# An ifftshift by DMA alone: the last strip split into small copies of 15 rows down to 2

## The chip, the cores and the metric

The kernel runs on one core of one Trainium2 chip. The metric is device time in microseconds (us), lower is better. A time is that of a whole execution; the profile is taken from one further execution, and its span runs from the first to the last instruction of the program. Nothing is computed: all work is done by the core's 16 DMA engines, which copy from one DRAM tensor to another.

## The reference

```python
def setup_inputs():
    return {"x": np.random.randn(8192, 8192).astype(np.float32)}

def reference(x):
    return np.fft.ifftshift(x)
```

For an even size this swaps the quadrants: element (r, c) of the output is element ((r + 4096) mod 8192, (c + 4096) mod 8192) of x. The tensor has 8192 rows of 32 KB, 268.4 MB in all, and each byte is read once and written once.

## The kernel before

R and C are 8192, hr and hc are 4096. A loop over `row` steps through the output in blocks of 512 rows, 16 blocks in all. In each block two DMAs are issued: the SP queue (`nc.sync`) copies the left half of the 512 output rows from the right half of the source rows, and the ACT queue (`nc.scalar`) copies the right half from the left half. Each DMA moves 512 half rows of 16 KB, 8 MB. Its access pattern, `dims`, has an outer dimension of 16 rows that follow each other (`ENGINES`), a middle one of 32 (`per`) with a step of 16 rows, and an inner one of 4096 contiguous floats.

So there are 32 DMAs, 16 on each queue, and no other work. The loop is inside a tile context, which does two things that are not seen in the code. It gives the DMAs eight semaphores in turn, four to each queue, and from the fifth DMA of a queue on it lets the issue wait until the DMA that last used the same semaphore has landed. And at the end it lets SP wait for all eight semaphores before the final barrier of the engines. Within a queue the DMAs run in the order of their issue; between the queues nothing sets an order.

Of the kernel before, what the change touches and what calls it, by code (L numbers as in the profile page):

```python
# [1 line left out]

# [4 lines left out]


ENGINES = 16


@with_exitstack
def kernel(
    ctx: ExitStack,
    tc: tile.TileContext,
    x: bass.AP,
    out: bass.AP,
):
    nc = tc.nc
    R, C = x.shape  # L20
    hr = R // 2
    hc = C // 2


    per = 32
    dims = [[C, ENGINES], [ENGINES * C, per], [1, hc]]
    for row in range(0, R, ENGINES * per):
        src_row = (row + hr) % R
        for queue, h in ((nc.sync, 0), (nc.scalar, hc)):
            queue.dma_start(  # L30
                out=bass.AP(out.tensor, out.offset + row * C + h, dims),
                in_=bass.AP(x.tensor, x.offset + src_row * C + hc - h, dims),
            )


# [1 line left out]
_INS = ['x']  # L37
_OUTS = [((8192, 8192), 'float32')]


def kernel(**inputs):
    import numpy as _np
    import concourse.bacc as _bacc
    import concourse.tile as _tile
    from concourse import mybir as _mybir
    from concourse.bass_utils import run_bass_kernel_spmd as _run

    nc = _bacc.Bacc("TRN2", target_bir_lowering=False, num_devices=1)  # L48
    arrays, args = {}, []
    for name in _INS:  # L50
        a = _np.ascontiguousarray(inputs[name])
        if a.dtype.kind in "iu":
            a = a.astype(_np.int64)
        arrays[f"in_{name}_dram"] = a
        args.append(nc.dram_tensor(f"in_{name}_dram", a.shape, _mybir.dt.from_np(a.dtype), kind="ExternalInput").ap())
    for i, (shape, dtype) in enumerate(_OUTS):
        dt = _mybir.dt.from_np(_np.dtype(dtype))
        args.append(nc.dram_tensor(f"out_{i}_dram", shape, dt, kind="ExternalOutput").ap())
    with _tile.TileContext(nc) as tc:
        kernel(tc, *args)  # L60
    r = _run(nc, [arrays], core_ids=[0])
    got = tuple(r.results[0][f"out_{i}_dram"] for i in range(len(_OUTS)))
    return got[0]
```

## Time and profile before

| what | value |
|---|---|
| three runs | 821.38, 823.50, 823.81 us; median 823.5 |
| span of the profiled execution | 821.2 us |
| DMAs | 16 on SP's queue (q1), 16 on ACT's (q10), 8192 KB each |
| median time from issue to landing | 204.0 us (SP), 204.1 us (ACT) |
| bytes moved | 268.44 MB, mean 327 GB/s |
| HBM read and written | 268.44 MB each, 654 GB/s over the span |

The profiled execution's own time is not given beside its span; the three times lie 0.2 to 2.6 us above it. A DMA is broken into packets, each of which is moved by one DMA engine. The profile has a record of each packet with its queue, bytes, start and duration, but not the number of its engine. A completion packet of 4 bytes raises a semaphore once an engine has done its share. The issuing instruction occupies only the queue of SP or ACT; it is not counted as busy time. In the view of stretches, PEclk is the clock of TensorE, which has no work here, the DMA share is the time of the packets that start in the stretch divided by sixteen times its length, and the rate counts their bytes.

### The profile page before, as it was taken

Reading aid. Unit: us, or ns where it says so; the run is one execution under the profiler, and the core shown is the slowest. Engines: PE = TensorE matmul, PEld = TensorE weight load, DVE = VectorE, ACT = ScalarE, POOL = GpSimd, SP = SyncE. Lnnn points to the kernel's source line nnn. Section 1 sums busy time; section 2 is a strip of 40 time slices with the busy share of each in tenths; the row PEclk is TensorE's granted clock in tenths of the full one; section 3 lists DMA queues with packets and bytes.
Section 4 is the critical chain, followed back from the end, with each engine's and each line's share of the span. In section 5 each row is a group of like instructions: output and inputs, shape, how many; then the busy total and the mean of one; then the engine's idle time right before and its main releaser. Section 6 shows DMA issues by size and latency. Waiting matters only on the chain. (4 is left out here: it accounts for less than half of the span.)

```text
span 821.2 us, 77 instructions
## 1 busy us (share of the span) xinstructions
POOL 0.2 (0%) x4
## 2 busy tenths in 40 slices
POOL 0000000000000000000000000000000000000000
DMA  8999999999999999999999999999999999999998
GB/s 296 333 324 329 331 328 334 330 330 329 327 330 329 331 326 332 332 327 328 330 330 330 330 323 330 324 330 330 332 326 329 330 322 333 329 329 327 330 329 276
DMA packets 16896, 268.44 MB, mean 327 GB/s; under 512 B 512, under 2 KB 512, under 8 KB 512
## 3 DMA queue, kind: packets, MB, share of 16 engines
q1 hardware_dynamic: 8448, 134.22, 50.2%
q10 hardware_dynamic: 8448, 134.22, 49.0%
HBM read 268.44 MB, written 268.44 MB: 654 GB/s over the span
## 5 line engine op out<-in xcount | busy, mean ns | idle before, releaser
L48 POOL MEMSET const-bfloat16-1.0<- 128x1 bf16 x1 | 0.1, 102 | 0.0
L48 POOL MEMSET const-uint8-127<- 128x1 uint8 x1 | 0.1, 102 | 0.0
L48 POOL MEMSET const-float32-0.0<- 128x1 f32 x1 | 0.1, 99 | 0.2 <-issue 0.2
L48 POOL MEMSET const-float32-1.0<- 128x1 f32 x1 | 0.1, 99 | 0.0
## 6 DMA issues: line engine op xcount, KB each, us to landing
out_dram<-in_x_dram ACTq DMA_DIRECT2D x16, 8192.0 KB, 204.1
out_dram<-in_x_dram SPq DMA_DIRECT2D x16, 8192.0 KB, 204.0
```

The costliest lines, as they stand in the source:

```text
L48: nc = _bacc.Bacc("TRN2", target_bir_lowering=False, num_devices=1)
```

## The change

The loop goes into a critical section of the tile context, in which the kernel does its own synchronization: every DMA raises one semaphore, `copied`, by 16 when it is done, and SP waits at the end until it has reached 16 times the number of DMAs, 62 x 16 = 992. The waits between the DMAs are gone.

SP's 16 DMAs are as before. ACT's first 15 are too. Its sixteenth is split. The first 384 rows of the last block go as one DMA of half rows (16 x 24 x 4096). Of the last 128 rows, one DMA moves the right 3584 floats of the half row (16 x 8 x 3584), and the strip that is left, 512 floats (2 KB) of each of the 128 rows, is moved by 29 DMAs: one of 9 rows, and then, for k from 15 down to 2, two of k rows each, the first with 256 + 8k floats of each row and the second with the other 256 - 8k. 9 + 15 + 14 + ... + 2 is 128.

```diff
+    with tc.tile_critical():
+        copied = nc.alloc_semaphore("copied")
+        n = 0
 
-    per = 32
-    dims = [[C, ENGINES], [ENGINES * C, per], [1, hc]]
-    for row in range(0, R, ENGINES * per):
-        src_row = (row + hr) % R
-        for queue, h in ((nc.sync, 0), (nc.scalar, hc)):
+        def copy(queue, row, col, dims):
+            nonlocal n
+            src = (row + hr) % R * C + (col + hc) % C
             queue.dma_start(
-                out=bass.AP(out.tensor, out.offset + row * C + h, dims),
-                in_=bass.AP(x.tensor, x.offset + src_row * C + hc - h, dims),
-            )
+                out=bass.AP(out.tensor, out.offset + row * C + col, dims),
+                in_=bass.AP(x.tensor, x.offset + src, dims),
+            ).then_inc(copied, 16)
+            n += 1
+
+        def halves(queue, row, rows, col, cols):
+            copy(queue, row, col, [[C, ENGINES], [ENGINES * C, rows // ENGINES], [1, cols]])
+
+        for row in range(0, R - 512, 512):
+            halves(nc.sync, row, 512, 0, hc)
+            halves(nc.scalar, row, 512, hc, hc)
+        row = R - 512
+        halves(nc.sync, row, 512, 0, hc)
+        halves(nc.scalar, row, 512 - LAST, hc, hc)
+        row = R - LAST
+        halves(nc.scalar, row, LAST, hc + PIECE, hc - PIECE)
+        copy(nc.scalar, row, hc, [[C, 9], [1, PIECE]])
+        row += 9
+        for k in range(15, 1, -1):
+            cut = 256 + 8 * k
+            copy(nc.scalar, row, hc, [[C, k], [1, cut]])
+            copy(nc.scalar, row, hc + cut, [[C, k], [1, PIECE - cut]])
+            row += k
+        nc.sync.wait_ge(copied, 16 * n)
```

`LAST` is 128 and `PIECE` is 512. In the built program the critical section also adds a signal from SP to ACT at its beginning, and at its end a signal from SP to ACT and one back.

## The prediction

> **What bounds the kernel now.** I read the page first. No engine computes; the only long work is DRAM to DRAM copying on two queues, q1 (SP's) and q10 (ACT's).
>
> ```profile
> span 821.2 us, 77 instructions
> ...
> DMA  8999999999999999999999999999999999999998
> ...
> DMA packets 16896, 268.44 MB, mean 327 GB/s; under 512 B 512, under 2 KB 512, under 8 KB 512
> ...
> q1 hardware_dynamic: 8448, 134.22, 50.2%
> q10 hardware_dynamic: 8448, 134.22, 49.0%
> ```
>
> The reader is to see that the 16 DMA engines are full from the second slice to the last but one: the two queue shares add to 99.2%. Of 16896 packets 512 are the small ones, one completion packet for each of 32 DMAs on 16 engines; the other 16384 carry 16 KB each. So only the ramp and the tail could be shorter; the body moves the same bytes through the same engines after the change.
>
> Next, the line that issues, for how early the queues are fed:
>
> ```profile
> engine op xcount: duration ns min/median/max, first and last start us, forms
> L30 ACTq DMA_DIRECT2D out_dram<-in_x_dram x16: 579/42036/48448, 0.7 to 618.8; - x16
> L30 SPq DMA_DIRECT2D out_dram<-in_x_dram x16: 571/41264/47309, 0.7 to 614.2; - x16
> ...
> DMA to landing us min/median/max: 51.6/204.0/207.1
> ```
>
> An issue that finds room takes 0.57 to 0.9 us. Most take some 42 us because the queue is full. ACT's last one starts at 618.8 and ends at 658.8, 161 us before its data has landed (820.3).
>
> Last, stretches of the tail (length, POOL busy, PEclk, DMA share, GB/s):
>
> ```profile
> 814.00:815.00 1.00, 0.00 (x0) 1.00 0.63 229
> 815.00:816.00 1.00, 0.00 (x0) 1.00 1.11 393
> 816.00:817.00 1.00, 0.00 (x0) 1.00 1.01 344
> 817.00:818.00 1.00, 0.00 (x0) 1.00 0.51 180
> 818.00:819.00 1.00, 0.00 (x0) 1.00 0.16 66
> 819.00:820.00 1.00, 0.00 (x0) 1.00 0.04 16
> 820.00:821.20 1.20, 0.00 (x0) 1.00 0.00 0
> ```
>
> After 817 the 16 engines run dry one by one: four packets start in 818 to 819 (66 KB), a single one after 819. By the semaphore records, ACT's last DMA lands on its first engine at 817.75 and on its last at 820.34, with a mean of 818.49. That skew, 1.85 us from mean to last, is all that a better balanced tail could win. From the last landing to the end is 0.85 us.
>
> The packet records (queue, bytes, start, duration) give the prices. A 16 KB packet never takes under 608 ns and most often 611 in the tail, or 26.8 GB/s on one engine; the mean under load is 795 ns. A completion packet takes 9 ns. On one engine the next packet starts 3 or 4 ns before the last one ends.
>
> **The change, part by part.** *Issues removed.* Before, from the fifth DMA of a queue on, each issue waits for the DMA four earlier (12 waits on each queue). Those waits go. They hid behind a full queue: at least three DMAs of 8 MB were queued behind each. Worth 0. Now the queue's own room paces SP and ACT, as it already paced their fourth issues: these ended at 47.1 and 51.7 us. SP's ended before any DMA had landed (first 50.8), so room comes back by packets and not by whole DMAs.
>
> *ACT's sixteenth DMA* becomes one of 384 rows, one of 128 rows without the strip (14336 B each, 8 on an engine) and 29 small ones. Bytes stay the same. On each engine 8 x 2 KB = 16 KB leave the big part: 0.61 us less at the tail's price.
>
> *The strip.* 9 rows whole, then for k = 15 to 2 two DMAs of k rows. That makes 9 + 2 x 119 = 247 data packets of 544 B to 2 KB and as many completion packets, plus 16 completions for the split: 510 packets more. Which engines they land on, no row shows. If rows were spread evenly each engine would carry 8 (0.61 us); if all fell on one, 256 KB would take 9.8 us. The nearest row is the 16 x 32 DMA, whose outer dimension of 16 became 16 engines with 32 packets each, so I take one row to one engine, every DMA starting at the same engine. Then the two heaviest carry 15 rows in 29 DMAs, the ninth 8 rows in 15, the fifteenth one row in 2, the last none.
>
> Price of a small data packet, from both sides: below, its bytes (76 ns for 2 KB); above, a cold packet. The first packets of the run took 0.94 to 1.40 us against 0.61, so 0.33 to 0.79 us each if nothing overlaps. It is nearest to the completion packet, which is small too and sits in a full queue: I take bytes plus 9 ns, and 9 ns for the completion. Heaviest engine: 15 x 0.076 + 29 x 0.018 = 1.67, less 0.61, is +1.06 us. Ninth: +0.27. Last: -0.61. Mean: +0.3 (510 x 9 ns / 16).
>
> The end moves by the engine that is last. If the staircase meets the skew (the last engine gets nothing), the end comes 0.61 us sooner. If it meets it the wrong way round, 1.06 us later. Landing times of the sixteen can't be tied to engine numbers, so I take no order: mean +0.3, and a little more because a maximum over shuffled loads grows, +0.5.
>
> *Issue of the strip.* 31 DMAs in place of one, 0.57 to 0.9 us each: 18 to 28 us on ACT's queue, nothing queued behind them but ACT's final drain. They must also wait for room: 29 x 2 packets on the fullest engine, at two data packets of about 0.8 us for each that ACT drains, is some 93 us on top of the 658.8. That ends near 752, before 815. The 161 us hide it; without that cover the 18 to 28 us would show.
>
> *One semaphore.* SP waits once for 992 = 62 x 16 instead of for eight semaphores. At start and end the critical section adds a few signals between SP and ACT. The end of before shows such a step at 30 to 80 ns: +0.1 us, from 0 to 0.3.
>
> Sum: 0 + 0.5 + 0.1 = +0.6 us on the span of 821.2, so 821.8. The three times shown lie 0.2 to 2.6 us above that span; on the median, 823.5 + 0.6 = 824.1 us.
>
> **A rule that speaks against it.** The last packet record ends at 819.996 and its landing is at 820.338; the first issue at 0.73 has its first packet at 2.19. A lone DMA thus costs about 1.8 us, yet DMAs queued in a row show none of it. The Trainium skill, "DMA: Bandwidth & Descriptors", section "Anatomy of one DMA", gives every DMA about 2.0 us of fixed cost, and its "Rules for kernel authors" say that transfers under 64 KB are mostly overhead. Taken in series, by an estimate from that page, 29 x 2.0 would give 58 us more, some 881 us. The same section says that the cost is completion latency and not set-up, which is why I don't take it so. Its section "Why a DMA increments its semaphore by 16 and not by 1" puts a DMA of k rows on the lowest-numbered k engines; no run here shows which they are.
>
> **Rivals.** *Serial completions (slower).* On the heaviest engine, 29 times a small write and its completion, with no other queue to fill the gap since q1 is done by then. If the next data packet waits until the completion has landed, each costs 0.34 us (record to landing): 29 x 0.34 + 1.15 - 0.61 = +10.4, minus 1.85 if that engine was an average one: 832 to 834. With a cold start of 0.6 on each, 841. For it: in before, every completion packet that I could follow in the body (394) had a packet of the other queue behind it, so the case isn't seen. Against it: the packet behind took 811 ns against 795, only 15 +/- 11 ns more. It decides from 0.13 us a DMA on (0.54 + 29 x 0.13 = 4.3, which is the slack of 1.85 and then 2.5).
>
> *Late issue (slower).* More than four DMAs were never outstanding on a queue. If the hardware holds four, 29 small DMAs of 1.8 us go four at a time after the big ones: 13 us, 837. Against it: SP's fourth issue ended at 47.1, by packets.
>
> *The staircase fits the skew (faster).* If the engines end in the order of their numbers and a small packet costs about 40 ns over its bytes, the stairs, 1.15 + 29 x 0.05 = 2.6 us high, match the skew of 2.6: up to 1.85 gained, 821.7. For it: the heights agree. Against: that is still within 0.3%, so more than the skew would have to go, a change of rate in the body, for which I see no cause.
>
> **How the numbers follow.** 0.3% is 2.5 us, about what a measurement of this kernel can tell from no change. Forecast (small packets flow, +0.6, or a partial fit): 0.55; its own range is 821.4 to 826, by the -0.6 to +2 of the two orders and the scatter of the three times. Serial completions 0.24, late issue 0.08: slower 0.32. Fit of the stairs and more: 0.13. The range from 820.6 to 836 takes in most of the first slow case and half of the fast one.
>
> **What would show it.** Body: mean GB/s near 330 in all slices, as before. Issue: ACT's last issue ends before 800. Tail: small packets of about 50 to 100 ns in a row on one engine; q10's last landing within 1.5 us of 820.3. Wrong if the last slices show several us at under 50 GB/s (serial), if ACT issues after 810 (late issue), or if the body's rate moves.

## The result, and the profile after

| | before | changed |
|---|---|---|
| median of 19 runs | 822.38 us (819.57 to 826.78) | 826.46 us (823.58 to 829.36) |
| ratio of the changed kernel to before | | 1.0047, 95% interval 1.0032 to 1.0063 |
| span of the profiled execution | 821.2 | 824.8 |

The change costs 0.47%, 3.9 us of 822.4, where +0.6 was forecast. The page of the changed kernel shows that the body moved at the same rate and that the difference lies in the last slice:

```profile
span 824.8 us, 112 instructions
...
GB/s 299 328 326 330 328 327 334 330 331 327 331 332 327 334 331 329 329 331 328 323 331 328 332 324 332 331 325 332 331 329 330 323 331 325 327 328 331 331 327 218
DMA packets 17406, 268.44 MB, mean 325 GB/s; under 512 B 775, under 2 KB 1013, under 8 KB 1022
...
q1 hardware_dynamic: 8448, 134.22, 50.0%
q10 hardware_dynamic: 8958, 134.22, 48.7%
```

There are 17406 - 16896 = 510 packets more, as counted in the prediction, and all are on q10. Before, the same row read:

```profile
GB/s 296 333 324 329 331 328 334 330 330 329 327 330 329 331 326 332 332 327 328 330 330 330 330 323 330 324 330 330 332 326 329 330 322 333 329 329 327 330 329 276
```

After the first slice all stay near 330 GB/s until the last, which falls to 218 where before had 276.

The line that issues, in the same columns as for before:

```profile
L33 ACTq DMA_DIRECT2D out_dram<-in_x_dram x46: 737/3177/109416, 0.9 to 800.3; - x46
L33 SPq DMA_DIRECT2D out_dram<-in_x_dram x16: 602/49277/110781, 1.0 to 603.5; - x16
```

ACT's last issue starts at 800.3 (and ends at 805.5 by its record), before the strip's first packet at 816.7. So the strip was in the queue in time. Then the stretches of the tail (length, POOL busy, PEclk, DMA share, GB/s):

```profile
816.00:817.00 1.00, 0.00 (x0) 1.00 0.92 341
817.00:818.00 1.00, 0.00 (x0) 1.00 0.91 274
818.00:819.00 1.00, 0.00 (x0) 1.00 0.60 101
819.00:820.00 1.00, 0.00 (x0) 1.00 0.26 28
820.00:821.00 1.00, 0.00 (x0) 1.00 0.07 5
821.00:822.00 1.00, 0.00 (x0) 1.00 0.01 1
822.00:823.00 1.00, 0.00 (x0) 1.00 0.00 0
823.00:824.80 1.80, 0.00 (x0) 1.00 0.00 0
```

Two things are to be seen. From 819 on some engines are still busy for 2 us (shares of 0.26, 0.07 and 0.01) but move almost nothing: 28, 5 and 1 GB/s. And after 821.3 no packet moves at all, yet the span goes on for 3.5 us. Before, the wait from the last packet (820.0) to the end was 1.2 us.

The packet and semaphore records tell what happens there. The last large packet ends at 818.87, sooner than before (819.99). The last packet of all ends at 821.27, its completion lands (raises the semaphore) at 823.65, and the last six landings come at 822.777, 822.952, 823.127, 823.303, 823.478 and 823.653: 175 ns apart, with nothing between. The difference of the two spans, 3.62 us, is made up so:

| stretch (us) | before | changed | difference |
|---|---|---|---|
| start to the end of the last large packet | 819.99 | 818.87 | -1.13 |
| from there to the last landing | 0.35 | 4.79 | +4.44 |
| from the last landing to the end | 0.85 | 1.15 | +0.30 |

The middle row is the measure that the experiments below use, as "tail". It doesn't contain the scatter of the body, which is several us from run to run. The small packets themselves show when the trouble begins. By the number of rows of a DMA, the median duration of its packets is:

```
rows      15   12   10    9     8     7     6     5     4     3     2
ns        46   46   46   56   172   179   188   190   187   189   187
```

The long and the short piece of a row differ by their bytes at first (64 and 28 ns for 15 rows), and later hardly: for 8 rows 768 B take 167 ns at the median and 1280 B 206, for 3 rows 928 B take 187 and 1120 B 191. Something with a fixed price of some 0.18 us a DMA has taken over from the bytes.

### The profile page after: what moved, and what is told of

It reads as the page before. It is cut to its first block, busy times and chain, and to the rows that moved or that the text cites. A ratio compares the mean times of both kernels' runs of the same rounds, so it can differ in the third digit from the quotient of the medians.

```text
span 824.8 us, 112 instructions
## 1 busy us (share of the span) xinstructions
POOL 0.2 (0%) x4
## 2 busy tenths in 40 slices
DMA packets 17406, 268.44 MB, mean 325 GB/s; under 512 B 775, under 2 KB 1013, under 8 KB 1022
```

## The experiments

The theory: an engine's completions land one after the other, each 0.17 to 0.18 us after the last. A number of them (13 or 14 by the records, 2.38 us from last packet to last landing over 0.175) can be pending while packets run ahead; then the packets are held to the same pace. The two fullest engines have 29 each, 29 x 0.175 = 5.1 us from the start of their strip. (In the profile of the kernel with five semaphores below, the strip's packets link up end to start, 3 ns apart, into 15 rows of 29, 29, 27, 25 and so on down to 4 and 2, so they lie on the engines as the prediction took them to.) Rivals: the critical section and its one semaphore; small packets or scarce descriptors; uneven load; a fixed cost of every DMA. Ratios are against runs of before on the same chip. All tails are of the one profiled execution of each kernel.

### One semaphore and no waits, without a strip

```diff
-        for row in range(0, R - 512, 512):
+        for row in range(0, R, 512):
             halves(nc.sync, row, 512, 0, hc)
             halves(nc.scalar, row, 512, hc, hc)
-        row = R - 512
...
```

After the loop this kernel has nothing but SP's wait.

> The 16 + 16 large DMAs of before, under one semaphore in the critical section; no strip. Serial completions (each DMA's completion on one engine takes 0.175 us and they land one after the other; in the changed kernel the last six landings are 175 ns apart): nothing to serialize, so before plus 0.5 us (first packet 0.24 us later, 0.30 us more after the last landing), ratio 1.0006. Rival, the cost lies in the one semaphore or in the missing waits between the DMAs: about the changed kernel's ratio, 1.0047, or 3 to 4 us over before.

Ratio 1.0009, interval 0.9986 to 1.0032; tail 0.35 us. The first packet starts at 2.37 us (2.19 in before) and the end comes 1.15 us after the last landing (0.85). So this part costs about 0.5 us, not 3.9; the median doesn't resolve it.

### The strip as one DMA

```diff
-        copy(nc.scalar, row, hc, [[C, 9], [1, PIECE]])
...
+        halves(nc.scalar, row, LAST, hc, PIECE)
```

> As the changed kernel, but the strip of 128 rows x 2 KB goes as one DMA over all 16 engines, 8 rows each. Serial completions: one completion more on each engine, 0.2 us; with the critical section's 0.5 us, before plus 0.5 to 0.8 us, ratio 1.0006 to 1.0010. Rival, splitting off 2 KB packets at the end costs by itself: 2 to 4 us over before.

Ratio 0.9997, interval 0.9973 to 1.0021; tail 0.92 us. 2 KB packets at the end are cheap when they share a completion: 128 of them, with a median of 84 ns.

### The same 512 B packets with 1 and with 32 completions on an engine

```diff
-PIECE = 512
+PIECE = 128
...
+        halves(nc.scalar, row, 512, hc + PIECE, hc - PIECE)
+        halves(nc.scalar, row, 512, hc, PIECE)
```

That is one DMA for the strip; in the other kernel the last line is 32 DMAs:

```diff
+        for r in range(row, R, ENGINES):
+            copy(nc.scalar, r, hc, [[C, ENGINES], [1, PIECE]])
```

> A strip of 512 B of each of the last 512 rows goes as one DMA: 32 packets of 512 B on each engine in a row at the end, with one completion each. Serial completions: the packets flow at some 28 ns each, 0.9 us for 256 KB as in bulk at 0.6; before plus 0.5 to 1.0 us, packets stay near 28 ns to the last. Rival, descriptors are supplied to an engine at some 95 ns each once the fetched ones are used up (the changed kernel's slow pairs of data and completion took 190 ns): the packets go to 95 ns after some 28, but with 33 descriptors it is hardly reached: plus 1 to 2 us, and packets of 95 ns are seen at the end.

> The same packets at the same addresses as in the kernel with one DMA for that strip, but as 32 DMAs of 16 rows: 32 completions on each engine. Serial completions: 32 x 0.175 = 5.6 us on every engine after its last large packet, also on the latest one: last landing 5 to 5.6 us later than with one DMA, before plus 5.5 to 6.5 us, ratio 1.007 to 1.008; at the end the landings of each engine are 175 ns apart. Rival, the cost is the uneven load of the low-numbered engines in the changed kernel: none here, before plus 1 us.

With one DMA: ratio 1.0020, interval 1.0000 to 1.0040, tail 1.05 us, packets of 27 ns at the median and at the 90th percentile. With 32: ratio 1.0064, interval 1.0040 to 1.0088, tail 5.89 us, packets of 178 ns from the 75th percentile on. The stretches of the tail, first with one DMA:

```profile
818.00:819.00 1.00, 0.00 (x0) 1.00 0.73 255
819.00:820.00 1.00, 0.00 (x0) 1.00 0.34 105
820.00:821.00 1.00, 0.00 (x0) 1.00 0.04 12
821.00:821.90 0.90, 0.00 (x0) 1.00 0.00 0
```

and then with 32:

```profile
821.00:822.00 1.00, 0.00 (x0) 1.00 1.08 53
822.00:823.00 1.00, 0.00 (x0) 1.00 0.93 23
823.00:824.00 1.00, 0.00 (x0) 1.00 0.26 5
824.00:825.00 1.00, 0.00 (x0) 1.00 0.06 2
825.00:826.00 1.00, 0.00 (x0) 1.00 0.00 0
826.00:827.00 1.00, 0.00 (x0) 1.00 0.00 0
827.00:828.70 1.70, 0.00 (x0) 1.00 0.00 0
```

In the second all engines are busy (1.08, 0.93) at 53 and 23 GB/s, which is the mark of the changed kernel, here on every engine. The bytes, packets and addresses are the same, so neither bytes, nor small packets, nor the uneven load makes the tail; the number of DMAs does, and with it the number of completions. That it is the completions shows after the last packet (824.69): nothing but landings goes on until 827.54. The pace is that of one engine and not of a place that all share: between 821 and 824, with most engines at it, 80 to 82 landings come in each us, some 5 for each of 16 engines or one in 0.2 us, and at the end a lone engine still needs 168 ns for one. Two things came out other than stated: the medians are 3.4 us apart and not 5 (the tails differ by 4.84), and the last landings are 168 ns apart, not 175.

### Half as many DMAs in the strip

```diff
-            copy(nc.scalar, row, hc, [[C, k], [1, cut]])
-            copy(nc.scalar, row, hc + cut, [[C, k], [1, PIECE - cut]])
+            copy(nc.scalar, row, hc, [[C, k], [1, PIECE]])
```

> The strip's pieces of k rows go whole, 15 DMAs in place of 29, over the same engines with the same bytes. Serial completions: 15 of them on the fullest engine, 15 x 0.17 = 2.6 us in place of 4.9 to 5.1; from the end of the last large packet to the last landing some 2.5 to 3 us (4.8 in the changed kernel, 0.35 in before); 2.4 us off the changed kernel, before plus 1 to 2 us. Rival, the number of bytes on the low-numbered engines sets the cost: no change, before plus 3.9.

Ratio 1.0012, interval 0.9987 to 1.0037: 1.0 us over before, as expected. The tail is 1.09 us, below the 2.5 to 3 expected: in this execution the last large packet ended on an engine with few rows, and the fuller engines had begun their strips earlier. The last landings are again 175 and 176 ns apart. The same bytes on the same engines with 15 completions in place of 29 cost little, so the bytes on the fullest engines don't set the price.

### The same strip, but not at the end

```diff
-        row = R - 512
-        halves(nc.sync, row, 512, 0, hc)
-        halves(nc.scalar, row, 512 - LAST, hc, hc)
         row = R - LAST
-        halves(nc.scalar, row, LAST, hc + PIECE, hc - PIECE)
...
         copy(nc.scalar, row, hc, [[C, 9], [1, PIECE]])
...
+        row = R - 512
+        halves(nc.sync, row, 512, 0, hc)
+        halves(nc.scalar, row, 512 - LAST, hc, hc)
+        row = R - LAST
+        halves(nc.scalar, row, LAST, hc + PIECE, hc - PIECE)
```

> The same DMAs, but the 29 of the strip are issued ahead of ACT's last two large pieces, so that a 16 KB packet of the other queue lies between two small ones on an engine. Serial completions: one per 0.6 us or more on an engine, under the 0.17 us that it takes, so hidden; from the last large packet's end to the last landing 0.35 us as before; before plus 0.3 to 0.8 us. Rival, 29 small DMAs cost their 4 us wherever they stand, since an engine does nothing else while a completion is pending: plus 3.5 to 4.5 us.

Ratio 1.0012, interval 0.9992 to 1.0032; tail 0.34 us. All 29 small DMAs are there, with their packets between 765.3 and 795.2 us, and the tail is that of before. A completion that is pending doesn't stop an engine that has large packets to move.

### 32 DMAs of large packets at the end

```diff
+        for r in range(row, R, ENGINES):
+            copy(nc.scalar, r, hc, [[C, ENGINES], [1, hc]])
```

> ACT's sixteenth DMA goes as 32 DMAs of 16 rows of 16 KB: 32 completions on each engine, as in the run of 32 small DMAs, but each with a packet of 16 KB (0.61 us alone). Serial completions: 0.17 us each under 0.61 us of data, hidden; before plus 0.3 to 0.8 us. Rival, a DMA has a fixed cost on the engine whatever its packets: 32 x 0.17 = 5.4 us more.

Ratio 1.0009, interval 0.9989 to 1.0029; tail 0.34 us. 32 completions on each engine cost nothing measurable when each has 16 KB ahead of it (0.61 us against 0.17). No fixed cost of a DMA shows.

### All on one queue

```diff
-        for row in range(0, R - 512, 512):
+        for row in range(0, R, 512):
             halves(nc.sync, row, 512, 0, hc)
-            halves(nc.scalar, row, 512, hc, hc)
...
+            halves(nc.sync, row, 512, hc, hc)
```

> All 32 large DMAs on SP's queue, none on ACT's. This asks whether the body has time to win: in the first 3 us of before, with one queue alone, packets of 16 KB took 0.61 to 0.66 us against 0.80 with both. If it is the alternation of two queues that slows an engine, about 0.65/0.80 of the time, 660 us. If it is memory under full load (the first packets meet no load yet), the same time, within 1%, 815 to 831 us; I expect this one.

Median 825.22 us, ratio 1.0035, interval 1.0012 to 1.0059. From the page:

```profile
DMA  9999999999999999999999999999999999999998
...
q1 hardware_dynamic: 16896, 268.44, 99.2%
```

One queue keeps the engines as full as two, and the time is 2.9 us longer, not 160 shorter. The alternation of queues doesn't set the rate of the body. What does is not shown: memory under full load is the reading of the expectation, and no run tests it by itself.

### The strip on four other semaphores

```diff
+            at = 1 + n % 4 if n > 32 else 0
...
-            ).then_inc(copied, 16)
+            ).then_inc(sems[at], 16)
```

SP then waits for the five counts.

> As the changed kernel, but the 29 DMAs of the strip raise four other semaphores in turn, the large ones keep the first. Serial per engine: an engine's completions still land 0.17 us apart, tail from the last large packet to the last landing 4 to 5 us, before plus 3.5 to 4.5 us. Rival, serial at the one semaphore that all 62 DMAs raise: with four of them the tail falls to a quarter, 1 to 1.5 us, before plus 0.5 to 1.5 us.

Ratio 1.0058, interval 1.0035 to 1.0080; tail 4.20 us, last landings 29, 142, 29, 140 and 173 ns apart: two engines taking turns, each at 169 to 173 ns. The ratio stands for 4.8 us over before, a little more than expected; its interval takes in the 3.5 to 4.5. The landings are serial on an engine, whichever semaphore they raise. That all are under one semaphore isn't what costs.

### One step of 16 rows on eight engines

```diff
...
+    copy(nc.scalar, R - 128, hc + piece, [[C, ENGINES], [ENGINES * C, 8], [1, hc - piece]])
+    copy(nc.scalar, R - 128, hc, [[C, 8], [8 * C, 16], [1, piece]])
```

The rest is as in before, with the tile context's own waits.

> Before without the critical section; the strip of 128 rows x 2 KB goes as one DMA over 8 rows at a time, so 16 packets (32 KB) on eight engines and none on the others, one completion each. If the low-numbered engines end earlier, as the one profile of the changed kernel suggests (large packets of the nine engines that got the first piece end 0.6 us sooner on average), the end comes 0.3 to 0.6 us sooner than in before; if the order of the engines is chance, 0 to 0.6 us later. Either is within what can be measured of the times: ratio 0.999 to 1.001.

Ratio 1.0013, interval 0.9992 to 1.0034. In its profile the tail is 1.62 us: small packets run on for 1.29 us after the last large one has ended. No gain from shifting bytes between engines is seen; one of 0.3 to 0.6 us would be too small to be told. No version tried beats before.

### The changed kernel again

> The changed kernel again, for a second profile of its tail and on the same chip as the kernel with five semaphores. Serial completions: last landings 0.17 us apart, 4.5 to 5.2 us from the last large packet to the last landing if a heavily loaded engine is late, down to 3.5 if it is early; before plus 3 to 5 us. Rival, the tail of the first profile was chance: under 2 us.

Ratio 1.0038, interval 1.0021 to 1.0056; tail 3.78 us. The last landings come in bunches of several engines, 8 to 12 ns apart within a bunch and 168 to 189 ns from one bunch to the next. In this execution a very late engine (its first strip packet at 820.46) was one with 15 packets and not 29, so the fullest ones had finished their large packets sooner. The tail follows the start of the strip on the fullest engine: 818.38 to 823.65 in the first profile, 5.27 us, against 29 x 0.175 = 5.1; here about 818.7 to 824.41, 5.7 us, with the slower pace of the bunches.

## Why the prediction was right or wrong, point by point

The measured 826.46 us lies within the stated range of 820.6 to 836, but that is no merit of the mechanism. The range had been drawn over most of the first slow rival as well; the sum was 824.1, and the forecast's own range, 821.4 to 826, ends below the measured time. The case that got a chance of 0.55, small packets that flow, is not what happened. What happened is the serial-completions rival, which got 0.24, at half its price. The prediction's own sign for it, last slices of several us at under 50 GB/s, came true: 28, 5, 1 and 0.

- *What bounds the kernel* held: the body's slices stayed near 330 GB/s and the change is in ramp and tail. So did the counting of 510 packets, and the removal of the waits at 0 as far as the run without a strip can tell it (1.0009, of which the signals at start and end make 0.0006).
- *Price of a small data packet*: the step that failed. "Bytes plus 9 ns, and 9 ns for the completion" described the records of the packets rightly at first (64 ns for 1504 B, 28 for 544 B, 9 for a completion). It took the record of a completion packet for the cost of the completion. The landings that follow come one at a time on an engine, 0.17 to 0.19 us apart. The +1.06 us of the fullest engine was +4.5 (5.1 less 0.61). What an engine spends the 0.17 us on, no run shows.
- *The serial-completions rival* was the right mechanism at the wrong price. It took the 0.34 us from record to landing for each. With 0.175 its own formula gives 0.54 + 29 x 0.175 = 5.6, less 1.85 of skew, is 3.8 us; measured, 3.9. That the two agree so well is partly luck: 0.5 of the 3.9 belongs to the signals at start and end, and the formula adds the 1.15 us of the bytes, which in fact were moved while completions were pending (5.27 us for all, 29 x 0.175 = 5.1). The evidence against it, 15 ns more after a completion in the body, didn't bear on it: there each completion had over 0.6 us until the next, so a price of 0.17 was hidden, as the strip placed earlier shows. The price of 0.175 lay above the 0.13 us a DMA from which this rival decides by the prediction's own sum.
- *Rule against row.* The 58 us more that the prediction estimated from a page's 2.0 us, taken in series, did not come; the whole change cost 3.9. The Trainium skill, "DMA: Bandwidth & Descriptors", section "Queues, rings and completion order", calls the raising of the semaphore a strongly ordered write, which lands only after every earlier write of that engine. The landings in single file agree. Its section "Anatomy of one DMA" calls the semaphore write nearly free, a bubble of about one cycle. That section, from which the 2.0 us are too, follows a DMA that GpSimd issues; those here are issued by SP and ACT. Among large packets the small DMAs were free as far as can be measured (1.0012); in a row at the end each cost 0.17 us, and the measurement decides.
- *Issue of the strip*: hidden, as said, but the cover was thinner. The pace of about two data packets per DMA held (3.1 us, 718.6 to 805.5), but the 9-row DMA's issue first took 59 us, which the prediction lacked, so that the last issue ended at 805.5 and not near 752. Of the 161 us of cover, 11 were left before the strip's first packet.
- *Late issue* fell: all 29 DMAs of the strip were issued by 805.5, before the first of their packets at 816.7.
- *One semaphore*: 0.5 us (0.24 at the start, 0.30 at the end) and not 0.1.
- *The staircase fits the skew*: not shown. In three profiles with the strip the engines that only get packets of the 15 to 10 row pieces began it 0.2 to 0.8 us later on average than the nine that get all from 9 rows up, but one of those nine was among the latest each time, not always the same one.

## What to carry to other kernels

When many small DMAs end a kernel, count the completions on the fullest engine, not the bytes: here each took 0.17 us in single file, 29 of them 5 us, whichever semaphore they raised. The same DMAs cost nothing that could be measured some 25 us before the end, where large packets ran beside them, and neither did the same bytes as one DMA. A packet record that ends isn't a landing: look at the time between the last packet and the last semaphore event.

## What was not expected of the hardware

By the records, completions are buffered: in the four profiles with a long tail the last packet was ahead of its landing by 2.3 to 2.85 us (13 to 17 completions), and packets had run freely before they slowed down to the pace of the landings. And without the waits between DMAs an issue can be held much longer than one DMA takes: the tenth on each queue took 109 to 111 us, and the DMA of 9 rows 59 us, with no effect on the engines.
